# The second norm's factor as a row for all partitions: two GpSimd transfers through DRAM in place of two transposes and a copy

## The chip, the cores and the metric

The kernel runs on one core of a Trainium2 chip. The metric is device time in microseconds (us) of one execution. The engines are TensorE (PE in the profile; its weight loads are PEld), VectorE (DVE), ScalarE (ACT), GpSimd (POOL) and SyncE (SP). SP, ACT and POOL can also issue DMA transfers; their queues are called SPq, ACTq and POOL's own.

## What is computed

One decoder layer over 256 tokens of width 1024: a first norm, a joint projection, two attention branches merged by gates, an output projection with a residual, then a second norm and a gated feed-forward part with a short convolution. The end of it is what matters here:

```python
x = x + jnp.einsum('bsd,de->bse', merged, w_out[l])
h2 = rms_norm(x, ffn_norm_g[l])
up = jnp.einsum('bsd,df->bsf', h2, w_ffn_up[l])
u, g = jnp.split(up, 2, axis=-1)
g = causal_depthwise_conv(g, ffn_conv_w[l], ffn_conv_b[l])
x = x + jnp.einsum('bsf,fd->bsd', jax.nn.silu(g) * u, w_ffn_down[l])
```

The second norm's factor is one number for each token, 1/sqrt(mean(x*x) + 1e-6). It doesn't depend on the feature, so it can be applied after the product with `w_ffn_up` just as well as before it, and the kernel does that.

## The kernel before

**Layout.** Products are made in two parts, high and low, of each operand. Weights come by SP transfers of 1 MB into `raw` (three buffers). ACT writes the high part `whi` (L134) and DVE the low part `wlo` (L135), each half of a transfer (128 x 1024) by itself; these halves are kept in the tiles `whi`/`wlo`, `qn`, `V` and `bias`, some eight halves ahead of the product that uses them. The order of PE is written out by hand in the code; the orders of DVE and ACT are decided by the scheduler when the program is built. PSUM holds eight banks, handed out by `bank()` and `banks()` (two at a time).

**The second norm.** `residual` (L591, L592) adds the output projection to x and sums the squares into `ssq`, tokens on the partitions. `norm2` (L636) makes of it `r2`, 128 partitions x 2: the factor of token 128 t + p stands in partition p, column t. Its last instruction is L203 on DVE.

**The feed-forward part.** Its 2816 channels are 22 blocks of 128, index `f`. For block `f` two banks take the two products u and g, with the *channels* on the partitions and the 256 tokens along the row (`up_half`, L662 with the high weights, L663 with the low). So the factor is needed as a row of 256 tokens that is the same in every partition: the tile `rs2`, called rsB in the profile. `norm2_row` (L643) made it: two PE transposes of `r2` against the identity (L646) into a bank, and a DVE copy from the bank to `rs2` (L647). It was called in the middle of the first two blocks, ahead of block 1's second half.

The first two blocks' products are interleaved (L746 to L749). After them, for each block in turn, `up_finish` empties the banks: ACT copies part of each (L677, `lows`), DVE adds (L678, `sq`), **DVE multiplies by the row (L679)**, ACT and DVE make the convolution (L683 to L685), ACT the silu (L686), DVE the product with u (L687), ACT the high part of the result (L691) and DVE its low part (L692), into `qT0`, `kT0` or `qT1` (qT and kT in the profile). Two blocks are one such tile, and `down(p)` multiplies the tile of blocks 2p and 2p+1 by a chunk of `w_ffn_down` (L709), the first block's part before the second's. `down(0)` stands in PE's order behind the products of block 4, `down(1)` behind block 6's, and so on.

```python
for f in range(NF):
    up_finish(f, first[f] if f < 2 else up_products(f))
    if f % 2 == 0 and f >= 4:
        down(f // 2 - 2)
```

**POOL.** Before, its last work is L305 at 18.5 us, a small product for the forget gate; no transfer is issued by it.

Of the kernel before, what the change touches and what calls it, by code (L numbers as in the profile page):

```python
# [8 lines left out]
F32 = mybir.dt.float32  # L9
# [8 lines left out]
P = 128  # L18
S = 256
NT = 2  # L20
# [21 lines left out]
def decoder_block(ctx, tc, a, out):  # L42
    nc = tc.nc
    sb = ctx.enter_context(tc.tile_pool(name="sb", bufs=1))
    ps = ctx.enter_context(tc.tile_pool(name="ps", bufs=1, space=PSUM))
    dr = ctx.enter_context(tc.tile_pool(name="dr", bufs=1, space=DRAM))
# [3 lines left out]
    def T(shape, tag, bufs=1, dt=F32):  # L50
        return sb.tile(shape, dt, tag=tag, bufs=bufs, name=tag)

    def bank():
        return ps.tile([P, 512], F32, tag="bank", bufs=8, name="bank")
# [86 lines left out]
    def use(c, h):  # L141
        if not state["hold"]:
            load(2 * pos[c] + h + state["ahead"])
        return split.pop((c, h))[:2]
# [42 lines left out]
    ident = cst[:, 0:128]  # L187
# [6 lines left out]
    def rsqrt_mean(dst, ss, n, shape, tag, bufs=2):  # L194

        w = T([P, 3] + shape, tag, bufs)
        v, y, t = w[:, 0], w[:, 1], w[:, 2]
        nc.vector.tensor_scalar(v, ss, 1.0 / n, EPS, op0=ALU.mult, op1=ALU.add)
        nc.scalar.activation(t, v, AF.Ln)
        nc.scalar.activation(y, t, AF.Exp, scale=-0.5)  # L200
        nc.vector.scalar_tensor_tensor(t, v, -0.5, y, op0=ALU.mult, op1=ALU.mult)
        nc.vector.tensor_tensor(t, t, y, op=ALU.mult)
        nc.vector.scalar_tensor_tensor(dst, t, 1.5, y, op0=ALU.add, op1=ALU.mult)  # L203
# [249 lines left out]
    def banks():  # L453
        return [bank() for _ in range(NT)]
# [115 lines left out]
    rs2 = T([P, S], "rsB")  # L570
# [58 lines left out]
    def last_turn():  # L629
        turn_x(1, 1)  # L630
        state["behind"] = split_h(1)
        state["hold"] = False
        load(2 * pos["wu", 0] + state["ahead"])
        state["behind"] = None

    def norm2():  # L636
        ss = T([P, NT], "ss2")
        nc.vector.tensor_tensor(ss, ssq[:, :, 0], ssq[:, :, 1], op=ALU.add)
        r2 = T([P, NT], "r2")
        rsqrt_mean(r2, ss, D, [NT], "rsv")  # L640
        return r2

    def norm2_row(r2):  # L643
        rp = bank()
        for t in range(NT):
            nc.tensor.transpose(rp[:, t * P:(t + 1) * P], r2[:, t:t + 1].to_broadcast([P, P]), ident)  # L646
        nc.vector.tensor_copy(rs2, rp[:, 0:S])  # L647


    acts = {}  # L650

    def up_half(f, h, two):
        if f == 1 and h == 1:
            norm2_row(r2)
        wh, wl = use(("wu", f), h)
        for i in range(2):
            for k4 in range(4):
                k = 4 * h + k4
                w = slice(k4 * 256 + i * P, k4 * 256 + (i + 1) * P)
                both = hx[:, k].rearrange("p a l t -> p (l t) a")  # L660
                high = hx[:, k, :, 0].rearrange("p a t -> p t a")
                nc.tensor.matmul(two[i], wh[:, w], both, start=(k == 0), stop=False)  # L662
                nc.tensor.matmul(two[i][:, 0:S], wl[:, w], high, start=False, stop=(k == KT - 1))  # L663
            if f == h == i == 0:
                last_turn()

    def up_products(f):
        two = banks()
        for h in range(2):
            up_half(f, h, two)  # L670
        return two
# [71 lines left out]
            nc.sync.dma_start(tail[:, at], fin[:, at])  # L743

    r2 = norm2()
    first = [banks(), banks()]  # L746
    for h in range(2):
        for f in range(2):
            up_half(f, h, first[f])  # L749
# [77 lines left out]
```

## Time and profile before

| | us |
|---|---|
| median of 3 runs (lowest, highest) | 351.95 (351.93, 352.18) |
| the profiled execution, its own time | 352.13 |
| its span, first to last instruction | 350.2 |
| granted TensorE clock, mean | 1.0 |
| `r2` complete (L203 ends) | 176.36 |
| row copied (L647 starts) | 185.45 |
| row first used (L679 starts) | 186.78 |

The span starts with the first instruction, and every moment below is counted from there. The profile lists for each engine how long it was busy, the chain of work that ended last (followed back from the last instruction to what released each step), and by the timeline every instruction with its start, its duration, its tiles as out<-in, and in square brackets how long its engine sat idle before it and what ended that.

### The profile page before, as it was taken

What the parts mean: (1) busy time and instruction counts of PE and PEld (TensorE: products, weight loads), DVE (VectorE), ACT (ScalarE), POOL (GpSimd) and SP (SyncE); (2) the same over time, 40 slices, a digit from 0 to 9 for tenths busy, and PEclk for the clock granted to TensorE, in tenths of its full rate; (3) what the DMA queues carried; (4) which work ended last, traced back from release to release, by engine and by line L of the source; (5) the groups of instructions that cost most, each with busy time, mean ns of one, the idle gap of its engine ahead of it and who ended that gap; (6) DMA issues with size and microseconds to landing.
All of it is one profiled execution on the core that took longest, in us unless ns stands there. A gap on an engine that the chain in (4) does not pass through costs nothing.

```text
span 350.2 us, 5361 instructions
## 1 busy us (share of the span) xinstructions
PE 345.5 (99%) x2023; PEld 302.2 (86%) x2023; DVE 283.7 (81%) x528; ACT 219.5 (63%) x388; POOL 1.3 (0%) x8
## 2 busy tenths in 40 slices
PE   8999999999999999999999999999999999999995
PEld 4888888888888888888899989989898999989885
DVE  5999989798697678995489999898878788797733
ACT  4967674868489475734496876775755656665420
POOL 0000000000000000000000000000000000000000
PEclk9999999999999999999999999999999999999999
DMA  7998885475560717576019656575565656450003
GB/s 261 411 343 288 318 302 196 167 254 228 159 262 1 240 31 249 204 306 254 41 60 359 196 226 240 209 273 172 196 232 182 191 227 210 160 233 2 0 0 122
DMA packets 14170, 70.10 MB, mean 200 GB/s; under 512 B 1592, under 2 KB 4800, under 8 KB 6720
## 3 DMA queue, kind: packets, MB, share of 16 engines
q1 hardware_dynamic: 12944, 68.69, 54.3%
q10 hardware_dynamic: 1200, 1.06, 0.9%
q8 instruction: 16, 0.26, 0.3%
q14 instruction: 10, 0.08, 0.1%
HBM read 68.69 MB, written 1.06 MB: 199 GB/s over the span
## 4 chain that ended last, share of the span: by engine, by line
PE 98%; DMA 1%; DVE 0%; issue 0%; ACT 0%; DVEq 0%
PE bank L245 30%; PE bank L662 22%; PE bank L709 16%; PE bank L663 11%; PE bank L539 6%; PE bank L587 6%; PE bank L382 2%; PE bank L423 2%; PE bank L409 1%; DMA g<-in_g 1%; PE bank L291 1%; PE bank L600 0%; PE bank L552 0%; PE bank L314 0%; PE bank L352 0%; DVE s L742 0%
## 5 line engine op out<-in xcount | busy, mean ns | idle before, releaser
L135 DVE TENSOR_TENSOR wlo<-raw,whi 128x1024 fp32r<-128x1024 f32 x94 | 114.2, 1221 | 21.0 <-ACT whi L134 20.8
L134 ACT ACTIVATE whi<-raw 128x1024 fp32r<-128x1024 f32 x94 | 97.9, 1055 | 43.8 <-PE bank L662 11.6
L662 PE MATMUL bank<-pp,whi 128*128 128x512 f32 x232 | 76.9, 383 | 0.0
L663 PE MATMUL bank<-pp,wlo 128*128 128x256 f32 x232 | 63.2, 273 | 0.0
L662 PEld LDWEIGHTS bank<-pp,whi 128*128 128x128 f32 x232 | 43.9, 189 | 6.0
L245 PE MATMUL bank<-whi,xh 128*128 128x512 f32 x160 | 48.4, 384 | 0.5 <-DVE xh L160 0.5
L245 PE MATMUL bank<-wlo,xh 128*128 128x512 f32 x160 | 47.8, 380 | 0.0
L245 PE MATMUL bank<-whi,xl 128*128 128x512 f32 x160 | 47.6, 379 | 0.0
L663 PEld LDWEIGHTS bank<-pp,wlo 128*128 128x128 f32 x232 | 44.5, 192 | 0.2
L245 PEld LDWEIGHTS bank<-whi,xh 128*128 128x128 f32 x160 | 29.6, 189 | 6.3 <-ACT whi L102 1.4
L245 PEld LDWEIGHTS bank<-wlo,xh 128*128 128x128 f32 x160 | 30.0, 189 | 4.8 <-DVE wlo L103 0.5
L245 PEld LDWEIGHTS bank<-whi,xl 128*128 128x128 f32 x160 | 30.2, 189 | 4.4 <-DVE xl L163 0.2
L709 PE MATMUL bank<-whi,qT 128*128 128x512 f32 (+1 forms) x92 | 27.8, 370 | 0.0
L678 DVE TENSOR_TENSOR sq<-bank,lows 128x256 f32<-128x256 f32 x44 | 18.2, 417 | 4.3 <-ACT lows L677 4.3
L677 ACT ACTIVATE lows<-bank 128x256 f32<-128x256 f32 x44 | 16.0, 369 | 8.2 <-PE bank L663 8.2
L709 PEld LDWEIGHTS bank<-whi,qT 128*128 128x128 f32 x92 | 17.2, 189 | 2.3
L662 PE MATMUL bank<-pp,bias 128*128 128x512 f32 x56 | 18.7, 382 | 0.0
L709 PE MATMUL bank<-wlo,qT 128*128 128x512 f32 (+1 forms) x46 | 17.0, 370 | 0.0
L539 PE MATMUL bank<-whi,pp 128*128 128x512 f32 x64 | 17.0, 382 | 0.0
L390 ACT ACTIVATE s<-s,nm 128x128 f32<-128x128 f32 (+1 forms) x32 | 14.1, 443 | 4.5 <-DVE nm L387 2.9
L679 DVE TENSOR_TENSOR sq<-sq,rsB 128x512 f32<-128x512 f32 x22 | 15.2, 689 | 0.6
L683 ACT ACTIVATE s<-sq,sm 128x256 f32<-128x256 f32 x22 | 13.0, 592 | 3.8 <-DVE sq L679 3.8
(168 smaller groups left out, 561.6 us busy)
## 6 DMA issues: line engine op xcount, KB each, us to landing
raw<-in_wu SPq DMA_DIRECT2D x22, 1024.0 KB, 4.8
raw<-in_wd SPq DMA_DIRECT2D x11, 1024.0 KB, 4.8
raw<-in_qkv SPq DMA_DIRECT2D x9, 1024.0 KB, 6.6
raw<-in_wg SPq DMA_DIRECT2D x8, 1024.0 KB, 4.8
raw<-in_wb SPq DMA_DIRECT2D x4, 1024.0 KB, 4.9
raw<-in_wo SPq DMA_DIRECT2D x4, 1024.0 KB, 4.8
lead<-in_lead SPq DMA_DIRECT2D x8, 384.0 KB, 5.7
raw<-in_qkv SPq DMA_DIRECT2D x2, 512.0 KB, 7.8
```

The source lines that it names most:

```text
L134: whi = nc.scalar.activation(hi, raw, AF.Copy)
L135: wlo = nc.vector.tensor_tensor(lo, raw, hi.bitcast(F32), op=ALU.subtract)
L245: nc.tensor.matmul(pt[t], lhs[:, k, t * P:(t + 1) * P], rhs, start=(k == 0 and i == 0), stop=(k == KT - 1 and i == 2))
L390: last_exp[:] = [nc.scalar.activation(s[:, j, c], s[:, j, c], AF.Exp, scale=-1.0, bias=nm[:, j, i:i + 1], accum_out=l[:, j, i:i + 1])]
L539: nc.tensor.matmul(ps_[t], lhs[:, t * P:(t + 1) * P], rhs, start=(k == 0 and i == 0), stop=(k == 3 and i == 2))
L587: nc.tensor.matmul(acc[t][dh], lhs[:, k, t * P:(t + 1) * P], rhs, start=(k == 0 and i == 0), stop=(k == KT - 1 and i == 2))
L662: nc.tensor.matmul(two[i], wh[:, w], both, start=(k == 0), stop=False)
L663: nc.tensor.matmul(two[i][:, 0:S], wl[:, w], high, start=False, stop=(k == KT - 1))
L677: nc.scalar.activation(lows[:, i:i + 1].rearrange("p b (a t) -> p b a t", a=2), apart(two[i][:, S:2 * S], 1), AF.Copy)
L678: nc.vector.tensor_tensor(halves(ev[:, i:i + 1]), apart(two[i][:, 0:S], 1), halves(lows[:, i:i + 1]), op=ALU.add)
L679: nc.vector.tensor_tensor(ev, ev, rs2[:, None, :].to_broadcast([P, 2, S]), op=ALU.mult)
L709: nc.tensor.matmul(o, lhs, rhs, start=(first and i == 0), stop=(end and i == 2))
```

## The change

The row is no longer made by PE. `r2` is written to a DRAM tile of 256 numbers by a transfer that POOL issues (token 128 t + p goes to place 128 t + p, so each number of four bytes is a piece of its own), and a second POOL transfer reads those 1024 bytes once for each of the 128 partitions into `rs2`. The call moves from the middle of the first two blocks to right behind `norm2`.

```diff
     def norm2_row(r2):
-        rp = bank()
-        for t in range(NT):
-            nc.tensor.transpose(rp[:, t * P:(t + 1) * P], r2[:, t:t + 1].to_broadcast([P, P]), ident)
-        nc.vector.tensor_copy(rs2, rp[:, 0:S])
+        row = dr.tile([S], F32, name="row")
+        nc.gpsimd.dma_start(row.rearrange("(t p) -> p t", t=NT), r2)
+        nc.gpsimd.dma_start(rs2, bass.AP(tensor=row.tensor, offset=row.offset, ap=[[0, P], [1, S]]))
...
     def up_half(f, h, two):
-        if f == 1 and h == 1:
-            norm2_row(r2)
         wh, wl = use(("wu", f), h)
...
     r2 = norm2()
+    norm2_row(r2)
     first = [banks(), banks()]
```

The order of PE around the place, before (bank_1890 is the second bank of block 0, bank_1891 the first of block 1):

```order
L662 MATMUL bank_1890<-pp_1698,whi_1707 128x512
L663 MATMUL bank_1890<-pp_1698,wlo_1708 128x256
L646 MATMUL bank_1987<-cst_174,r2_1881 128x128 x2
L662 MATMUL bank_1891<-pp_1698,whi_1765 128x512
L663 MATMUL bank_1891<-pp_1698,wlo_1766 128x256
```

And after (its lines from here on have numbers lower by 3; the same two banks are 1893 and 1894):

```order
L660 MATMUL bank_1893<-pp_1698,wlo_1708 128x256
L659 MATMUL bank_1893<-pp_1698,whi_1707 128x512
L660 MATMUL bank_1893<-pp_1698,wlo_1708 128x256
L659 MATMUL bank_1894<-pp_1698,whi_1765 128x512
L660 MATMUL bank_1894<-pp_1698,wlo_1766 128x256
```

The two transposes and their bank are gone, and the rest of PE's order is the same to the end of the program.

The order of DVE where the row is first used, before (L135 are low halves of weights, L678 the sums of blocks 0 and 1, L679 block 0's product with the row):

```order
L135 TENSOR_TENSOR qn<-raw,qn 128x1024
L135 TENSOR_TENSOR wlo<-raw,whi 128x1024 x2
L647 COPY rsB<-bank 128x256
L678 TENSOR_TENSOR sq<-bank,lows 128x256 x3
L679 TENSOR_TENSOR sq<-sq,rsB 128x512
L135 TENSOR_TENSOR wlo<-raw,whi 128x1024 x2
L684 SCALAR_TENSOR_TENSOR s<-sq,sm,s 128x255
```

And after:

```order
L135 TENSOR_TENSOR qn<-raw,qn 128x1024
L135 TENSOR_TENSOR wlo<-raw,whi 128x1024 x2
L675 TENSOR_TENSOR sq<-bank,lows 128x256 x3
L676 TENSOR_TENSOR sq<-sq,rsB 128x512
L135 TENSOR_TENSOR wlo<-raw,whi 128x1024 x2
L681 SCALAR_TENSOR_TENSOR s<-sq,sm,s 128x255
```

The copy is gone, and the first product with the row (L679, now L676) waits for the second transfer instead.

A little later on DVE, up to the low part of block 1 (the second qT row), before:

```order
L685 SCALAR_TENSOR_TENSOR s<-sq,sm,s 128x254
L692 TENSOR_TENSOR qT_2024<-s,qT_2024 128x256
L678 TENSOR_TENSOR sq<-bank,lows 128x256
L135 TENSOR_TENSOR V<-raw,V 128x1024
L687 TENSOR_TENSOR s<-sq,s 128x256
L679 TENSOR_TENSOR sq<-sq,rsB 128x512
L135 TENSOR_TENSOR bias<-raw,bias 128x1024
L692 TENSOR_TENSOR qT_2024<-s,qT_2024 128x256
```

And after:

```order
L682 SCALAR_TENSOR_TENSOR s<-sq,sm,s 128x254
L675 TENSOR_TENSOR sq<-bank,lows 128x256
L689 TENSOR_TENSOR qT_2023<-s,qT_2023 128x256
L676 TENSOR_TENSOR sq<-sq,rsB 128x512
L135 TENSOR_TENSOR V<-raw,V 128x1024
L684 TENSOR_TENSOR s<-sq,s 128x256
L681 SCALAR_TENSOR_TENSOR s<-sq,sm,s 128x255
L135 TENSOR_TENSOR bias<-raw,bias 128x1024
L689 TENSOR_TENSOR qT_2023<-s,qT_2023 128x256
```

Here the scheduler puts block 2's steps earlier, and one of them (L684, now L681) stands ahead of block 1's low part where it stood behind it. ACT's order changes in the same stretch in the same manner, one step of block 2 ahead of block 1's L691; further on both engines keep the order of before. On POOL the two transfers stand behind L305 with nothing behind them but the program's end. SP's order doesn't change.

## The prediction

> **What bounds the kernel.** I read the chain of work that ended last first, since it says whose time is the kernel's time, and beside it the busy times:
>
> ```profile
> PE 345.5 (99%) x2023; PEld 302.2 (86%) x2023; DVE 283.7 (81%) x528; ACT 219.5 (63%) x388; POOL 1.3 (0%) x8
> PE 98%; DMA 1%; DVE 0%; issue 0%; ACT 0%; DVEq 0%
> ```
>
> PE is 98% of the chain. The 1% of DMA is the first load. What another engine does costs time only where PE comes to wait for it, so next I look at the stretches around the change (window in us, its length, then busy time and instructions of each engine, the granted clock, the DMA share, GB/s):
>
> ```profile
> 176.00:187.00 11.00, 11.00 (x71) 10.12 (x70) 10.35 (x17) 9.34 (x16) 0.00 (x0) 1.00 0.44 165
> 187.00:200.00 13.00, 13.00 (x82) 11.94 (x81) 12.52 (x20) 11.62 (x19) 0.00 (x0) 1.00 0.71 265
> 200.00:220.00 20.00, 20.00 (x111) 18.02 (x110) 19.63 (x36) 12.91 (x25) 0.00 (x0) 1.00 0.62 214
> ```
>
> PE has no gap in any of them. DVE, the third figure, is nearly as full: 10.35 of 11, 12.52 of 13, 19.63 of 20 us. PE sets the pace here, but a DVE that loses time from 187 on gets little of it back before 220. POOL does nothing.
>
> **What goes from PE.** The timeline of PE around the transposes (start, duration):
>
> ```profile
> 181.52 0.38 PE L662 MATMUL bank<-pp,whi 128*128 128x512 f32 x1
> 181.74 0.27 PE L663 MATMUL bank<-pp,wlo 128*128 128x256 f32 x1
> 181.85 0.38 PE L646 MATMUL bank<-cst,r 128*128 128x128 f32 x2
> 181.99 0.46 PE L662 MATMUL bank<-pp,whi 128*128 128x512 f32 x1
> 182.28 0.27 PE L663 MATMUL bank<-pp,wlo 128*128 128x256 f32 x1
> 182.39 0.38 PE L662 MATMUL bank<-pp,whi 128*128 128x512 f32 x1
> ```
>
> Matmuls overlap, so their cost is the distance between starts, not their duration. A pair of L662 and L663 takes 181.85 - 181.52 = 0.33 us where nothing stands behind it. From 181.52 to 182.39 there are two pairs, 0.66 us, but 0.87 us pass. The two transposes cost **0.21 us** of PE: 0.14 until the next L662 starts, and 0.07 more until its L663. With PE on the chain from here to the end, all of it leaves the time, unless PE meets a wait later that it doesn't meet now.
>
> **What goes from DVE and moves there.**
>
> ```profile
> 176.20 0.16 DVE L203 SCALAR_TENSOR_TENSOR r<-rsv 128x2 f32<-128x2 f32 x1
> ...
> 178.63 1.23 DVE L135 TENSOR_TENSOR wlo<-raw,whi 128x1024 fp32r<-128x1024 f32 x1 [0.46 <-ACT whi L134]
> 179.78 1.22 DVE L135 TENSOR_TENSOR V<-raw,V 128x1024 fp32r<-128x1024 f32 x1
> ...
> 185.45 0.41 DVE L647 COPY rsB<-bank 128x256 f32<-128x256 f32 x1
> 185.79 1.07 DVE L678 TENSOR_TENSOR sq<-bank,lows 128x256 f32<-128x256 f32 x3
> 186.78 0.68 DVE L679 TENSOR_TENSOR sq<-sq,rsB 128x512 f32<-128x512 f32 x1
> 187.38 2.35 DVE L135 TENSOR_TENSOR wlo<-raw,whi 128x1024 fp32r<-128x1024 f32 x2
> 189.65 0.48 DVE L684 SCALAR_TENSOR_TENSOR s<-sq,sm,s 128x255 f32<-128x255 f32 x1
> 190.04 0.42 DVE L678 TENSOR_TENSOR sq<-bank,lows 128x256 f32<-128x256 f32 x1
> ...
> 196.18 0.42 DVE L678 TENSOR_TENSOR sq<-bank,lows 128x256 f32<-128x256 f32 x1
> ...
> 199.72 0.42 DVE L692 TENSOR_TENSOR qT<-s,qT 128x256 fp32r<-128x256 f32 x1
> ```
>
> The copy cost 185.79 - 185.45 = 0.34 us between starts. DVE is off the chain, so I count nothing for it; if it did hold PE up somewhere unseen, 0.34 us is the most it can give. Without it the first product with the row (L679) is due at 186.78 - 0.34 = 186.44. Of the changed order, L684 now stands ahead of block 1's low part. That is a step of 190.04 - 189.65 = 0.39 us by the L684 above, about what the copy gave back, so I leave the 199.72 of that low part where it is.
>
> With one bank fewer asked for, later pairs of banks are handed out one place further round, and PE's waits for an emptied bank move with them. I cost that at nothing: the sums that empty the banks of blocks 1 and 2 (L678) run from 190.04 to 196.18 + 0.42, and `down(0)`, the next to ask for four banks at once, starts at 200.41 (its row is below). Were that cover gone, PE would wait for one L678, 0.42 us.
>
> **How much time the row has.** `r2` is complete at 176.20 + 0.16 = 176.36. POOL is idle, its queue is empty, so the first transfer starts at once. The row is needed at 186.44, **10.1 us** later. What if it is later still? Behind L679 on DVE stand two low halves of weights, then the whole rest of blocks 0 and 1; on ACT L683 waits for L679, with the high halves behind it. All of that moves as one. What PE needs first of it is the tile of blocks 0 and 1 in `down(0)`:
>
> ```profile
> 200.41 0.38 PE L709 MATMUL bank<-whi,qT 128*128 128x512 f32 x1
> 202.78 0.59 PE L709 MATMUL bank<-whi,qT 128*128 128x512 f32 x2
> 203.43 0.59 PE L709 MATMUL bank<-whi,qT 128*128 128x512 f32 x2
> ```
>
> Each of its products is three matmuls, high by high, high weights' low part, then the low part of block 0 or 1, and the first four of them (12 matmuls from 200.41) use block 0. So block 1's low part is read first by the matmul that starts at 203.43, and by 0.21 less, 203.22, after the change. L692 delivers it at 199.72 + 0.42 = 200.14. The cover is 203.22 - 200.14 = **3.1 us**, so PE begins to wait only when the row lands after 186.44 + 3.1 = **189.5**, that is 13.2 us behind `r2`. The halves of weights behind L679 have more: the two low halves at 187.38, done at 189.73, are the chunk of that same `down(0)`, 200.41 - 189.73 = 10.7 us or more ahead.
>
> **What the two transfers take.** No row shows a transfer issued by POOL, nor one in pieces of four bytes. The nearest rows, with KB and median us from issue to landing, and the pair of transfers that ACT issues for the forget gate's bias in the same pattern (a row to DRAM, then from there to all partitions):
>
> ```profile
> g<-in_g ACTq DMA_DIRECT2D x1, 4.0 KB, 3.2
> wfr<-in_wf SPq DMA_DIRECT2D x1, 32.0 KB, 8.6
> out<-s SPq DMA_DIRECT2D x2, 128.0 KB, 2.1
> bias<-cd ACTq DMA_DIRECT2D x1, 1024.0 KB, 5.7
> 58.40 0.52 ACTq L357 DMA_DIRECT2D cd<-pT  x1
> 61.96 0.40 ACTq L358 DMA_DIRECT2D bias<-cd  x1
> ```
>
> First transfer, 1 KB in 256 pieces: `g` is 128 partitions with small pieces at 3.2 us, `wfr` has more and waits behind other loads, 8.6 us. The pair waits on itself as ours does: the second is issued 61.96 - 58.40 = 3.56 us after the first, which went to DRAM too. I take 3.6, with 3.2 and 8.6 as ends. Second transfer, 128 pieces of 1 KB: `out<-s` moves the same 128 KB in the same pieces, 2.1 us; `bias<-cd` has the same kind of source, eight times the data and 5.7 us. I take 2.1, with 2.1 and 5.7 as ends. Sum: 5.7, with ends 5.3 and 14.3; the row lands at **182.1**, with ends 181.7 and 190.7. That is 4.3 us ahead of the first need, and 7.4 ahead of the point where PE would wait; what making descriptors on POOL costs more than on ACT or SP has that much room.
>
> From the Trainium skill's page "DMA: Bandwidth & Descriptors", section on the anatomy of a DMA on the gpsimd path, about 2.0 us fixed and bytes over 436 GB/s, an estimate would be 2.0 + 2.3 = 4.3 us and a landing at 180.7; no run here shows such a transfer yet.
>
> The transfers also find the DMA engines free at first (columns as above, the last two DMA share and GB/s):
>
> ```profile
> 176.00:179.00 3.00, 3.00 (x21) 2.76 (x20) 2.35 (x7) 2.72 (x6) 0.00 (x0) 1.00 0.00 0
> 179.00:181.00 2.00, 2.00 (x14) 1.84 (x13) 2.00 (x3) 2.00 (x3) 0.00 (x0) 1.00 0.00 0
> 181.00:183.00 2.00, 2.00 (x15) 1.84 (x14) 2.00 (x2) 2.00 (x3) 0.00 (x0) 1.00 0.41 74
> 183.00:185.00 2.00, 2.00 (x14) 1.84 (x13) 2.00 (x3) 1.27 (x5) 0.00 (x0) 1.00 1.02 430
> ```
>
> They are idle until 181 and full from 183 on. A second transfer that is late runs into that load, and 128 KB at 430 GB/s hold it up by 0.3 us in turn; the low half that follows it is for 200.41.
>
> **The sum.** The profiled execution took 352.13 us (1.93 around its span of 350.2). Less 0.21 it is 351.92. The median, 0.18 below that execution, goes the same way: 351.95 - 0.21 = **351.74**. That is 0.06% less, where a measurement of this kernel tells some 0.2% (0.7 us) from no change.
>
> **Rivals.**
>
> *The row is late* (the one that ends slower). Place: L679 on DVE, then PE at the fifth product of `down(0)`. Price: the landing less 189.5, no more and no less, since DVE has next to nothing to catch up with. By the upper ends, 190.7, it is 1.2 us: 351.74 + 1.2 = 352.9. It is slower by over 0.7 us from a landing at 190.4. Against it: both transfers would have to take the far ends. For it: no row has POOL issue anything.
>
> *DVE keeps POOL from making the descriptors.* DVE runs without a gap from 178.63 to 186.44. If the second transfer's descriptors could be written only once DVE stands still at L679, it lands at 186.44 + 2.1 to 5.7, 188.5 to 192.1, and PE loses 0 to 2.6 us: up to 354.3. What bears on it is POOL's one product:
>
> ```profile
> 18.32 0.69 DVE L182 TENSOR_TENSOR bias<-bias 128x512 f32<-128x512 f32 x1
> 18.51 0.65 POOL L305 TENSOR_TENSOR wf<-wfr,g 128x64 f32<-128x64 f32 x1 [17.33 <-DMA wfr<-in_wf]
> ```
>
> It started inside a DVE product of two SBUF tiles and took 0.65 us for 64 columns, ending 0.15 after it: held up by one instruction at most, not by the next. DVE starts a new instruction every 179.78 - 178.63 = 1.15 us in our window, so a hold of that kind costs a transfer about one of them, which the 7.4 us cover. The Trainium skill's page "SBUF — State Buffer", section "Who interferes with whom", says that DVE and GpSimd share a pair of SBUF ports, that a DVE copy or tensor_scalar in a two-port mode shuts GpSimd, and so its DMAs, out, and that tensor_tensor has no such mode. By that rule this case's window, which holds only two-input operations, is safe; the rows above can't tell more.
>
> *The new queue costs something before or behind the work.* The program gains a third issuer of transfers. Now 1.93 us lie outside the span with two of them (SP and ACT); half of that, 0.97, is the most I give a third: 351.74 + 0.97 = 352.7. At the other end it is free, as the forecast has it.
>
> *Nothing arrives at the end, or a little more does.* Should PE meet a wait later, 0.21 is lost and the time stays at 351.95. Should DVE's 0.34 count as well, it is 351.4. That the change doesn't do what it says can be set aside: the orders show the two transfers on POOL and no transposes.
>
> **How the numbers follow.** Row hidden, 0.21 gained: 0.79, at 351.74. Nothing or a little more arrives: 0.07, 351.4 to 351.95. Row late by itself: 0.06, to 352.9. POOL kept out by DVE: 0.04, to 354.3. New queue: 0.04, to 352.7. The time is 351.74. The range goes from 351.4, all of DVE's gain, to 352.9, the far ends of both transfers, and leaves out about 0.06. Faster by over 0.2% needs more than all that is removed: 0.02. Slower by over 0.2% takes most of the three late or costly cases: 0.10. Within 0.2%: 0.88.
>
> **What would show it.** The next L662 should start 0.33 us behind the one before where L646 stood. L679's row should show no idle time put down to the transfer into rsB, and start near 186.4. The second transfer should land near 182. PE should be gapless at the first L709. If L679 waits but `down(0)` shows no gap, the cover of 3.1 us is right and only the transfers were mis-sized; a gap there puts the first rival right, by its size. If the span shrinks by 0.21 and the time doesn't, it is the queue.

## The result, and the profile after

The kernel with the change takes **356.46 us** (median of 4 runs, 356.38 to 356.99), and the kernel before, run beside it, 352.04 us (351.93 to 352.18). The ratio is 1.0126 with a 95% interval of 1.011 to 1.0141: the change makes the kernel slower by 4.4 us. The forecast was 351.74 us, and the range ended at 352.9. One execution of the kernel before, beside the experiments, took 518.99 us at a mean clock of 0.656 and is left out of the medians below.

The first view again is the page's busy times and the chain of work that ended last:

```profile
PE 347.6 (98%) x2021; PEld 303.4 (86%) x2021; DVE 283.0 (80%) x527; ACT 219.6 (62%) x388; POOL 2.8 (1%) x10
PE 88%; issue 3%; DVE 3%; DMA 3%; ACT 1%; POOL 0%; DVEq 0%; POOLq 0%; ACTq 0%
```

PE, 98% of the chain before, is now 88%. Ten points have gone to a detour, and the chain names it: POOL's first transfer, 9.13 us of "issue" behind it, 7.51 us of the transfer into rsB, then DVE's work up to the third matmul of `down(0)`. The detour in order, from the timelines of POOL, DVE and PE (start, duration, and in brackets the idle time before and what ended it) and the page's DMA issues (KB, median us from issue to landing):

```profile
176.49 0.88 POOL L645 DMA_DIRECT2D row<-r  x1 [157.13 <-DVE r L203]
186.53 0.58 POOL L646 DMA_DIRECT2D rsB<-row  x1 [9.15 <-DMA row<-r]
row<-r POOLq DMA_DIRECT2D x1, 1.0 KB, 9.7
rsB<-row POOLq DMA_DIRECT2D x1, 128.0 KB, 7.5
194.13 0.69 DVE L676 TENSOR_TENSOR sq<-sq,rsB 128x512 f32<-128x512 f32 x1 [7.78 <-DMA rsB<-row]
194.74 2.35 DVE L135 TENSOR_TENSOR wlo<-raw,whi 128x1024 fp32r<-128x1024 f32 x2
206.73 0.42 DVE L689 TENSOR_TENSOR qT<-s,qT 128x256 fp32r<-128x256 f32 x1
202.34 0.48 PE L706 MATMUL bank<-whi,qT 128*128 128x512 f32 x1 [2.18 <-ACT qT L688]
203.27 0.84 PE L706 MATMUL bank<-whi,qT 128*128 128x512 f32 x2 [0.23 <-DVE qT L689]
204.33 1.06 PE L706 MATMUL bank<-whi,qT 128*128 128x512 f32 x2
207.65 0.59 PE L706 MATMUL bank<-whi,qT 128*128 128x512 f32 x2
```

The write of 1 KB takes 9.7 us. The second transfer can't be issued before 186.53, about when the product with the row was due, and lands 7.5 us later at 194.04. DVE, which before had no gap here, stands still for 7.78 us, and everything behind L676 moves with it. PE comes to `down(0)` at about 200.2; it starts it at 202.34 and goes on at 203.27, after waits of 2.18 and 0.23 us for the two parts of block 0. Then its matmuls get longer: 1.06 us where the same pair takes 0.59. The windows show why (window, length, PE, PEld, DVE, ACT, POOL, granted clock, DMA share, GB/s):

```profile
202.00:204.00 2.00, 1.43 (x5) 0.92 (x6) 2.00 (x6) 1.96 (x5) 0.00 (x0) 0.92 0.81 262
204.00:206.00 2.00, 2.00 (x6) 1.59 (x5) 2.00 (x4) 2.00 (x5) 0.00 (x0) 0.50 0.62 262
206.00:208.00 2.00, 2.00 (x8) 1.68 (x7) 2.00 (x5) 1.28 (x3) 0.00 (x0) 0.72 0.28 33
```

The granted clock falls to half for 3.4 us, from 203.7 on. In these three windows PE does 2 x (0.08 + 0.50 + 0.28) = 1.7 us less work than at the full clock. The wait of 2.41 us and this 1.7 us make 4.1 of the 4.5 us that were lost there (the span grew from 350.2 to 354.5, and PE had 0.21 less to do).

The row is not the only thing that is late. The windows that showed the DMA engines idle and then full before:

```profile
179.00:181.00 2.00, 2.00 (x15) 1.84 (x13) 2.00 (x3) 2.00 (x3) 0.00 (x0) 1.00 0.00 0
181.00:183.00 2.00, 2.00 (x15) 1.84 (x14) 2.00 (x2) 2.00 (x3) 0.00 (x0) 1.00 1.49 33
183.00:185.00 2.00, 2.00 (x15) 1.84 (x14) 2.00 (x3) 1.36 (x5) 0.00 (x0) 1.00 0.24 41
180.84 0.33 SPq L131 DMA_DIRECT2D raw<-in_wd  x1
191.75 2.00 ACT L134 ACTIVATE whi<-raw 128x1024 fp32r<-128x1024 f32 x2 [6.90 <-DMA raw<-in_wd]
```

From 183 to 185 they moved 430 GB/s before and move 41 now. SP issued the 1 MB of `w_ffn_down` (`wd`) at 180.84 as before, but ACT can start on it only at 191.75, 10.9 us later. Before, the same two moments were 181.02 and 185.92, 4.9 us apart:

```profile
181.02 0.33 SPq L131 DMA_DIRECT2D raw<-in_wd  x1
185.92 2.01 ACT L134 ACTIVATE whi<-raw 128x1024 fp32r<-128x1024 f32 x2 [0.65 <-DMA raw<-in_wd]
```

So two things are late, the row and a load, and either could be what PE waits for.

### The profile page after: what moved, and what is told of

It reads as the page before. It is cut to its first block, busy times and chain, and to the rows that moved or that the text cites. A ratio compares the mean times of both kernels' runs of the same rounds, so it can differ in the third digit from the quotient of the medians.

```text
span 354.5 us, 5357 instructions
## 1 busy us (share of the span) xinstructions
PE 347.6 (98%) x2021; PEld 303.4 (86%) x2021; DVE 283.0 (80%) x527; ACT 219.6 (62%) x388; POOL 2.8 (1%) x10
## 3 DMA queue, kind: packets, MB, share of 16 engines
q10 hardware_dynamic: 1200, 1.06, 0.9%
HBM read 68.82 MB, written 1.06 MB: 197 GB/s over the span
## 4 chain that ended last, share of the span: by engine, by line
PE 88%; issue 3%; DVE 3%; DMA 3%; ACT 1%; POOL 0%; DVEq 0%; POOLq 0%; ACTq 0%
PE bank L245 30%; PE bank L659 17%; PE bank L706 17%; PE bank L660 8%; PE bank L539 6%; PE bank L587 5%; DMA rsB<-row 2%; PE bank L382 2%; PE bank L423 2%; DVE wlo L135 1%; PE bank L409 1%; DMA lead<-in_lead 1%; PE bank L291 1%; ACT sq L592 0%; PE bank L552 0%
## 5 line engine op out<-in xcount | busy, mean ns | idle before, releaser
L135 DVE TENSOR_TENSOR wlo<-raw,whi 128x1024 fp32r<-128x1024 f32 x94 | 114.3, 1222 | 19.2 <-ACT whi L134 18.9
L706 PE MATMUL bank<-whi,qT 128*128 128x512 f32 (+1 forms) x92 | 29.2, 386 | 2.4 <-ACT qT L688 2.2
L706 PEld LDWEIGHTS bank<-whi,qT 128*128 128x128 f32 x92 | 18.0, 198 | 5.7 <-ACT qT L688 2.5
L676 DVE TENSOR_TENSOR sq<-sq,rsB 128x512 f32<-128x512 f32 x22 | 15.2, 691 | 8.4 <-DMA rsB<-row 7.8
L706 PE MATMUL bank<-wlo,qT 128*128 128x512 f32 (+1 forms) x46 | 17.8, 387 | 0.0
```

The lines of the kernel that those rows point to most:

```text
L135: wlo = nc.vector.tensor_tensor(lo, raw, hi.bitcast(F32), op=ALU.subtract)
L676: nc.vector.tensor_tensor(ev, ev, rs2[:, None, :].to_broadcast([P, 2, S]), op=ALU.mult)
L706: nc.tensor.matmul(o, lhs, rhs, start=(first and i == 0), stop=(end and i == 2))
```

## The experiments

Three questions were open. Does the write take 9.7 us because of who issues it, or because of its pattern of 256 pieces of four bytes (theory P in the expectations; S is the form of it that closely packed small writes wait on each other)? Does the late load cost time by itself (L), or only the late row? And what would the change have been worth with neither?

**The issuer.** The first transfer issued by ACT instead of POOL:

```diff
-        nc.gpsimd.dma_start(row.rearrange("(t p) -> p t", t=NT), r2)
+        nc.scalar.dma_start(row.rearrange("(t p) -> p t", t=NT), r2)
```

> The first transfer (the factor to DRAM, 256 pieces of 4 bytes) is issued by ACT instead of POOL; the second stays on POOL. Theory P (the pieces): four-byte writes to DRAM are slow whoever issues them, so the first transfer lands again 9 to 10 us after its issue, the row near 194, and the time is 355.5 to 356.8. Rival Q (the issuer): making the transfer on POOL was what took long; then it lands 3 to 4 us after its issue, as the other small ACT transfers do, the row by 188, and the time is 351.7 to 352.2.

Measured: 355.85 us (354.96 to 356.71; ratio 1.0099, interval 1.007 to 1.0128). The kernel before, beside this run and the next three, has a median of 351.94 us. The DMA issues, and DVE's first product with the row:

```profile
row<-r ACTq DMA_DIRECT2D x1, 1.0 KB, 9.7
rsB<-row POOLq DMA_DIRECT2D x1, 128.0 KB, 7.0
193.21 0.69 DVE L676 TENSOR_TENSOR sq<-sq,rsB 128x512 f32<-128x512 f32 x1 [6.96 <-DMA rsB<-row]
```

ACT's transfer takes the same 9.7 us. The issuer is not the cause.

**The pattern.** The same numbers, laid out in DRAM as token p, then token 128 + p, so that each partition writes one piece of eight bytes. DVE's product with the row reads them in that order:

```diff
-        nc.gpsimd.dma_start(row.rearrange("(t p) -> p t", t=NT), r2)
+        nc.gpsimd.dma_start(row.rearrange("(p t) -> p t", t=NT), r2)
...
-        nc.vector.tensor_tensor(ev, ev, rs2[:, None, :].to_broadcast([P, 2, S]), op=ALU.mult)
+        ev4 = ev.rearrange("p i (t c) -> p i t c", t=NT)
+        nc.vector.tensor_tensor(ev4, ev4, rs2.rearrange("p (c t) -> p t c", t=NT)[:, None].to_broadcast([P, 2, NT, P]), op=ALU.mult)
```

> As the change, but the DRAM row is laid out partition by partition, so the first transfer writes 128 pieces of 8 bytes instead of 256 of 4; the first product with the row reads it through a rearranged view. Theory P: half the pieces, about half of the 9.7 us, so it lands near 181.3, the second transfer is ahead of the big load issued at 180.84 and lands by 185, and the time is 351.7 to 352.1. Rival Q: nothing in it changes for the issuer, 9.7 and 7.5 us stay, 356.4.

Measured: 352.0 us (351.51 to 352.59, 10 runs; ratio 0.9997, interval 0.9983 to 1.001), no different from the kernel before. Its DMA issues and DVE rows:

```profile
row<-r POOLq DMA_DIRECT2D x1, 1.0 KB, 3.7
rsB<-row POOLq DMA_DIRECT2D x1, 128.0 KB, 5.7
186.94 0.80 DVE L677 TENSOR_TENSOR sq<-sq,rsB 128x512 f32<-128x512 f32 x1
191.19 2.36 DVE L135 TENSOR_TENSOR wlo<-raw,whi 128x1024 fp32r<-128x1024 f32 x2 [3.46 <-ACT whi L134]
```

Twice the piece, half their number, and the write takes 3.7 us; the row is there when DVE asks for it. The load is still late: the low half of `wd` waits 3.46 us. But PE's list of waits has none for it; the matmul that reads block 1's low part, at 203.85, comes about 0.2 us behind its place in the row of matmuls.

**The load by itself.** The kernel before, with its transposes and copy, and the two transfers added to it, into a tile that nobody reads:

```diff
+        row = dr.tile([S], F32, name="row")
+        nc.gpsimd.dma_start(row.rearrange("(t p) -> p t", t=NT), r2)
+        nc.gpsimd.dma_start(T([P, S], "spare"), bass.AP(tensor=row.tensor, offset=row.offset, ap=[[0, P], [1, S]]))
         return r2
```

> The kernel before, with its transposes and copy, and the two POOL transfers of the change issued at the same place into a tile that nothing reads. Theory W (only the wait for the row costs): the time is that of before, 351.9 to 352.3. Rival L (the first transfer also holds up the weight loads behind it): the load issued at 181 lands near 191.7 again instead of 185.9, ACT's and DVE's halves of it are then 5 to 6 us late with block 0's and block 1's later steps queued behind them, 2 to 3 us more than the cover of 3.1, so 354 to 355.

Measured: 354.93 us (354.4 to 355.37; ratio 1.0073, interval 1.0049 to 1.0096). The timelines of DVE and PE:

```profile
187.12 0.68 DVE L682 TENSOR_TENSOR sq<-sq,rsB 128x512 f32<-128x512 f32 x1
193.16 2.36 DVE L135 TENSOR_TENSOR wlo<-raw,whi 128x1024 fp32r<-128x1024 f32 x2 [5.36 <-ACT whi L134]
202.12 0.48 PE L712 MATMUL bank<-whi,qT 128*128 128x512 f32 x1 [1.20 <-ACT qT L694]
206.45 0.70 PE L712 MATMUL bank<-whi,qT 128*128 128x512 f32 x2 [0.86 <-DVE qT L695]
```

The product with the row (L682) is on time, and the kernel still loses 3.0 us. What is late is the low half of `wd` right behind it: it stands in DVE's queue ahead of all that remains of blocks 0 and 1, so PE waits for their tile (`qT`), not for the weights. The late load without the late row is worth 3.0 us; the change loses 4.4, and the 1.4 between them are left for the late row and the change's other differences. The interval here goes from 1.7 to 3.4 us, so the shares are rough.

**The first transfer alone.** The same, without the second transfer (the line with `spare` left out):

> The kernel before (transposes and copy kept) with the first transfer alone added, behind r2's last instruction, into DRAM that nobody reads. Theory (the crowded write holds up the loads by itself): the transfer takes 8 to 10 us, wd's load lands at 190 or later, its high half on ACT waits 5 us or more, and the time is 354 to 355, as with both transfers unused (354.93). Rival (it is the second transfer, 128 KB, that stands ahead of the loads): wd's load lands by 187 as before and the time is 352.0 to 352.5.

Measured: 354.15 us (353.44 to 354.95; ratio 1.0057, interval 1.0037 to 1.0077). The write in the page's DMA issues, the step of the chain that stands for the load (start, duration), and the longer of PE's two waits (the other, 0.69 us, ends at 201.00):

```profile
row<-r POOLq DMA_DIRECT2D x1, 1.0 KB, 9.3
180.77 10.35 DMA raw<-in_wd
205.33 0.70 PE L711 MATMUL bank<-whi,qT 128*128 128x512 f32 x2 [0.86 <-DVE qT L694]
```

A write of 1 KB that nobody reads makes a load of 1 MB take 10.35 us instead of 4.9 and costs the kernel 2.05 us. The trace's record of single DMA packets, in the kernel with the change, shows the shape of it: the write's own packets left within 0.2 us at 178.0, but the first eight packets of `wd`, 8 KB each, took 4.1 to 6.8 us, and the nine after them 0.7 to 0.8. In the kernel before, the first eight took 1.1 to 1.3 us.

**The most that there was to gain.** No row at all: no transposes, no copy, no transfers, `rs2` filled with ones early by POOL.

```diff
+    nc.gpsimd.memset(rs2, 1.0)
...
-        if f == 1 and h == 1:
-            norm2_row(r2)
```

> The kernel before without the row: no transposes, no copy, no transfers; the tile holds ones from the start, so the second norm's factor is left out. It measures the gain that the change could have had at most. Forecast by the distances between matmuls: 0.21 us less than before, 351.75 to 351.95. Rival: the gain doesn't reach the end, 352.0 to 352.1; or DVE's 0.34 us counts as well, 351.5.

Measured: 351.85 us (351.38 to 352.26, 10 runs; ratio 0.9993, interval 0.9982 to 1.0003). That is 0.1 us below the kernel before, which can't be told from nothing by the medians. The profiled executions tell more: counted from the end of `r2` to the end of the span, this one is 0.23 us shorter than the kernel before, close to the 0.21 worked out for the two transposes.

**Probes of the write.** The write in several forms, and the second transfer, were timed by themselves: the kernel before with transfers that nobody needs, one after the other, from 317 us on, where few loads run. First who issues, and the size of the piece: `da` and `db` are 256 pieces of four bytes in the change's pattern, by POOL and by SP; `dc` is 128 pieces of eight.

> The kernel before, with three transfers to DRAM that nothing reads added one behind the other from about 316 us on, where the DMA engines have no load left: da, the factor's pattern (256 pieces of 4 bytes) issued by POOL; db, the same issued by SP; dc, 128 pieces of 8 bytes issued by POOL. Theory P (four-byte pieces in this order are slow, whoever issues): da and db both land 9 to 10 us after issue, dc in 3 to 4. Rival Q2 (slow only beside other loads): all three land in 3 to 4 us here.

```profile
da<-src POOLq DMA_DIRECT2D x1, 1.0 KB, 8.2
db<-src SPq DMA_DIRECT2D x1, 1.0 KB, 8.0
dc<-src POOLq DMA_DIRECT2D x1, 1.0 KB, 3.4
```

The pattern is slow with the DMA engines quiet, and from SP as from POOL. Next, `da` with the 256 pieces of four bytes 512 bytes apart, `rowt` the change's second transfer by itself, from constants, and `db` 128 KB back to DRAM:

> The kernel before, with three POOL transfers that nothing needs added from about 316 us on, in the quiet: da, 256 pieces of 4 bytes as in the change, but each 512 bytes apart in DRAM; rowt, the second transfer's pattern (1 KB of DRAM read once for each of 128 partitions); db, 128 pieces of 1 KB to DRAM. Theory S (many small writes into the same few short stretches of DRAM wait on one another): da lands in 3 to 4 us. Rival N (each small piece costs by itself, wherever it lies): da lands in 9 to 10 us. For rowt: 2 to 3 us if its 7.5 us in the changed kernel came from the loads beside it, 5 or more if reading one place 128 times is slow by itself. db: 2 to 3 us.

```profile
rowt<-in_consts POOLq DMA_DIRECT2D x1, 128.0 KB, 3.2
db<-rowt POOLq DMA_DIRECT2D x1, 128.0 KB, 2.0
da<-src POOLq DMA_DIRECT2D x1, 1.0 KB, 2.1
```

Spread out, the same pieces take 2.1 us. So neither POOL nor the four bytes as such cost anything, and the second transfer alone takes 3.2 us, not 7.5. Next the order and the number: `da` four-byte pieces in the order of the partitions, `db` only 128 of them in 512 bytes, `dc` 256 pieces of eight bytes in 2 KB.

> The kernel before, with three POOL transfers to DRAM that nothing needs added from about 316 us on: da, 256 pieces of 4 bytes in the order of the 8-byte pieces (both numbers of a partition next to each other); db, 128 pieces of 4 bytes, tokens next to each other; dc, 256 pieces of 8 bytes in the factor's order. If the number of pieces decides: da and dc 9 to 10 us, db 3 to 5. If the size of a piece decides: da 9 to 10, db 5, dc 3 to 4. If the order decides (neighbours in DRAM written by the same DMA engine or by several): da 3 to 4, db as half of the change's transfer, 5, and dc 9 to 10.

```profile
da<-src POOLq DMA_DIRECT2D x1, 1.0 KB, 7.5
db<-src POOLq DMA_DIRECT2D x1, 0.5 KB, 7.6
dc<-src POOLq DMA_DIRECT2D x1, 2.0 KB, 3.9
```

The order doesn't matter (7.5 us here, 8.2 in the first probe), and half the pieces take as long, which none of the three theories had. This left open whether it is the size of a piece or how many share a stretch of DRAM. In the last probe all pieces have four bytes, 8, 32 and 64 bytes apart:

> A probe on the kernel before, in the stretch from 317 us where few loads run: POOL writes the same 256 numbers of four bytes to DRAM three times, one after the other, at a distance of 8 bytes (da), 32 bytes (db) and 64 bytes (dc). Nobody reads them. If what counts is how many pieces share a stretch of DRAM, da takes 3.4 to 5 us, as 8-byte pieces side by side do (64 pieces in 512 bytes), db 2.3 to 2.8, dc 2.1 to 2.5. If it is that a piece has four bytes rather than eight, all three take 7 to 8 us, or the time falls only where a number has some larger block (32, 64 bytes) to itself. Time of the kernel: 351.7 to 352.3.

```profile
da<-src POOLq DMA_DIRECT2D x1, 1.0 KB, 3.8
db<-src POOLq DMA_DIRECT2D x1, 1.0 KB, 2.0
dc<-src POOLq DMA_DIRECT2D x1, 1.0 KB, 2.0
```

At a distance of 8 bytes they take 3.8 us, as 256 pieces of eight bytes side by side do (3.9), and from 32 bytes on 2.0. So it is how densely the pieces lie: 4 bytes apart 7.5 to 8.2 us, 8 apart 3.4 to 3.9, and at 32, 64 and 512 bytes 2.0 to 2.1. Between 8 and 32 bytes nothing was measured.

**The change with this one thing altered.** The write's pieces 512 bytes apart, the rest of the change as it is, with a second transfer of the same size and pattern that reads constants; the second norm's factor is left out by that:

```diff
-        row = dr.tile([S], F32, name="row")
-        nc.gpsimd.dma_start(row.rearrange("(t p) -> p t", t=NT), r2)
-        nc.gpsimd.dma_start(rs2, bass.AP(tensor=row.tensor, offset=row.offset, ap=[[0, P], [1, S]]))
+        row = dr.tile([S, P], F32, name="row")
+        nc.gpsimd.dma_start(row.rearrange("(t p) c -> p t c", t=NT)[:, :, 0:1], r2[:, :, None])
+        nc.gpsimd.memset(r2, 1.0)
+        nc.gpsimd.tensor_copy(rs2[:, 0:NT], r2)
+        c = a["consts"]
+        nc.gpsimd.dma_start(rs2, bass.AP(tensor=c.tensor, offset=c.offset, ap=[[0, P], [1, S]]))
```

> The change with one thing altered: the first transfer writes r2's 256 numbers of four bytes 512 bytes apart in DRAM, so that no two share a short stretch. POOL then overwrites r2 and copies it into the row's tile, so that it waits for that transfer as before, and the second transfer reads 1 KB of the constants for all partitions; the second norm's factor is left out by that. Theory (the crowded four-byte writes are the whole loss, as themselves and by the loads that they hold up): first transfer 2 to 3 us, second 3 to 6 us, wd's load lands by 188, the product with the row starts before 188 with little or no wait, time 351.7 to 352.3. Rival (some of the loss is the second transfer's, 128 KB through the same DMA engines as the loads, or the changed order of DVE and ACT): the product with the row waits until 190 or later, or the halves of wd do, and the time is 353 or more.

Measured: 351.99 us (351.62 to 352.53, 10 runs; the kernel before beside it 352.1; ratio 0.9997, interval 0.9987 to 1.0006). Its DMA issues and DVE's rows:

```profile
row<-r POOLq DMA_DIRECT2D x1, 1.0 KB, 2.1
rsB<-in_consts POOLq DMA_DIRECT2D x1, 128.0 KB, 4.8
186.23 0.68 DVE L679 TENSOR_TENSOR sq<-sq,rsB 128x512 f32<-128x512 f32 x1
188.65 2.36 DVE L135 TENSOR_TENSOR wlo<-raw,whi 128x1024 fp32r<-128x1024 f32 x2 [1.74 <-ACT whi L134]
```

All of the loss is gone, with the changed orders of DVE and ACT, the two waits of POOL and the 128 KB still there. The product with the row starts at 186.23 without a wait. The second transfer, now issued ahead of the loads' bulk, still makes `wd` 1.6 us late (its low half waits 1.74 us), but that is hidden. The time is inside what was expected, and the rival (353 or more) falls.

No version beat the kernel before. By the run without a row there are some 0.2 us to gain, below what the medians can tell apart, and both harmless forms of the change (pieces of eight bytes, which computes the same as before, and spread-out pieces, which leaves the factor out) stand where the kernel before stands.

## Why the prediction was wrong

**What PE gains: right.** The timeline of PE in the changed kernel, where the transposes stood:

```profile
181.33 0.38 PE L659 MATMUL bank<-pp,whi 128*128 128x512 f32 x1
181.65 0.38 PE L659 MATMUL bank<-pp,whi 128*128 128x512 f32 x1
181.98 0.38 PE L659 MATMUL bank<-pp,whi 128*128 128x512 f32 x1
```

The pairs follow each other at 0.32 and 0.33 us, and behind `r2` the run without a row is 0.23 us shorter, the one with spread-out pieces 0.18, for the 0.21 forecast. The medians are too coarse to show it.

**DVE's copy at nothing, the changed order, the banks: right.** The kernel with spread-out pieces has the same three changes and loses nothing. It gains no more than the transposes give, so the 0.34 us of the copy were indeed off the chain.

**The first transfer: the step that failed first.** It was put at 3.6 us with 8.6 as the far end, and took 9.7. The nearest rows were chosen by the number of small pieces and by the bytes. What decided was how densely the pieces lie in DRAM, which none of the three rows shares. `g<-in_g` and `wfr<-in_wf` read from DRAM, and `cd<-pT` writes 8 KB there, in eight rows of 1 KB. The Trainium skill's page "DMA: Bandwidth & Descriptors", in the section "Anatomy of one DMA", gives about 2.0 us fixed plus the bytes at 436 GB/s: the spread-out writes (2.0 and 2.1 us) agree, the dense one takes about four times that in the quiet (7.5 to 8.2) and almost five times beside loads (9.7). The Trainium skill's page "DMA: Bandwidth & Descriptors", section "Specifications", says that below 512 bytes the engine does a read-modify-write. That would fit writes that wait on each other, but pieces 32 bytes apart share such a stretch too and took 2.0 us; why density has this effect stays open.

**The second transfer: mis-sized, as a consequence.** It was put at 2.1 to 5.7 us and took 7.5. By itself it takes 3.2, beside loads on time 4.8, and 7.5 when the late write sends it off behind the load that it has held up: its first packet starts at 191.33, 4.8 us behind its issue, where with spread-out pieces that took 1.4. Together the landing came at 194.04, where the far end was 190.7.

**"128 KB at 430 GB/s hold it up by 0.3 us": the step that failed in kind.** The prediction asked only what the second transfer would do to the loads. The 1 KB of the first held up 1 MB on another queue by over 5 us, with 2.05 us of loss by itself.

**The 10.7 us that the weight halves were given: wrong in the same place.** That is the cover of the product that reads those halves. But in DVE's order they stand ahead of the remaining steps of blocks 0 and 1, so a late half has only the cover of what is queued behind it, the 3.1 us of block 1's low part. The prediction had worked out those 3.1 us for the row and didn't give them to the load whose halves stand right behind it.

**The cover of 3.1 us and the price: right, and they carry over to every run.** Below is the moment at which block 1's low part is complete, counted from the end of `r2` (23.78 us in the kernel before: 199.72 + 0.42 - 176.36), and the price by the prediction's rule, lateness less 3.1, less 0.21 where the transposes are gone. Against it stand the time from the end of `r2` to the end of the span in the same execution, less that of the kernel before (350.25 - 176.36 = 173.89 us; for the change 354.51 - 176.18 = 178.33), and the median less that of the kernel before beside it.

| run | low part later by | rule | same execution, behind `r2` | medians |
|---|---|---|---|---|
| no row | -0.2 | -0.2 | -0.2 | -0.1 |
| pieces 512 bytes apart | 1.70 | -0.2 | -0.2 | -0.1 |
| pieces of eight bytes | 3.25 | -0.1 | 0.2 | 0.1 |
| write alone, not read | 5.38 | 2.3 | 2.3 | 2.05 |
| both transfers, not read | 5.91 | 2.8 | 2.8 | 3.0 |
| first transfer by ACT | 6.37 | 3.1 | 3.1 | 3.9 |
| the change | 7.19 | 3.9 | 4.4 | 4.4 |

In the execution that gave the lateness the rule is within 0.3 us in every run but the change, and mostly within 0.1. The medians scatter around it: the profiled execution of the first transfer by ACT was the fastest of three, 354.96 us. For the change the rest is the clock. Block 1's low part was ready at 207.15, and PE came for it only at 207.65, without a wait, having lost 1.7 us at half speed. At the full clock it would have come at about 206.0 and waited until 207.15; so the clock cost 207.65 - 207.15 = 0.5 us more than that wait, the difference between 3.9 and 4.4.

The place of the wait was one step off: the prediction looked for it at the fifth product of `down(0)`, where block 1's low part is read, and PE stood first at the first one, for block 0. Block 0's high part, complete at 195.81 before, has a cover of some 4.4 us, more than block 1's 3.1, but over 7 us of lateness use up both. With the first transfer by ACT, where the clock stayed at 1.00, PE waits at both places:

```profile
201.42 0.48 PE L706 MATMUL bank<-whi,qT 128*128 128x512 f32 x1 [1.34 <-ACT qT L688]
206.28 0.70 PE L706 MATMUL bank<-whi,qT 128*128 128x512 f32 x2 [0.48 <-DVE qT L689]
```

By the prediction's own price, the landing less 189.5, a landing at 194.04 gives 4.5 us and 356.3, nearly what was measured. That is luck in part: DVE did get back some 0.6 us up to block 1's low part (3.9 by the table, not 4.5), and the clock took about as much away.

**The rivals.** The row being late was given 0.06 and 352.9: the right mechanism, with the price cut off at rows that don't show this write, and without the late load, which by itself costs 2.05 to 3.0 us in the runs. That DVE keeps POOL from making descriptors falls: the write's packets left at 178.0, 1.5 us behind the issue at 176.49 and long before DVE stood still, and ACT's transfer was as slow. With spread-out pieces the second transfer too was issued while DVE ran without a gap, at 179.99, and landed 4.8 us later, before DVE's next gap. The new queue at the program's end costs nothing: 356.38 - 354.5 = 1.9 us lie outside the span, as before.

## What to carry to other kernels

A factor spread over the partitions should not be written to DRAM as neighbouring four-byte pieces: give each partition one longer piece, or space them by 32 bytes, and the same transfer takes 2 to 4 us instead of 7.5 to 9.7. A transfer that is small in bytes can still hold up a load on another queue, so the price of an added transfer is looked for in the next load's landing too. And the cover of a late input is not that of its last reader but that of the first thing queued behind it on an engine that works in order.

## What the runs showed that was not expected

Writes of a few bytes that lie 4 bytes apart in DRAM take 7.5 to 8.2 us in the quiet and 9.3 to 9.7 beside loads, whether 128 or 256 of them and whoever issues; 8 bytes apart 3.4 to 3.9, and from 32 bytes on 2.0 to 2.1. While such a write was under way, the first packets of a load on another queue, 8 KB each, took 4.1 to 6.8 us instead of 1.1 to 1.3.

In the change PE's granted clock fell to 0.50 for 3.4 us after waits of 2.18 and 0.23 us, and PE did 1.7 us less work in it. With the first transfer by ACT, four waits of 1.34, 0.22, 0.33 and 0.48 us, spread over some 6 us, left it at 1.00. The Trainium skill's page "TensorE: Matmul & The Clock Gate", section "Part 1: The HAM clock gate", puts the fall behind an idle window of about 3.4 us; here a shorter wait was enough, while the 3.4 us at half speed agree.
